# A mixer-and-FFN layer: another buffer for the recurrence's decay, another ring for the last pooling copies, a later place for one chunk's products

## The chip, the cores and the metric

The kernel runs on one core of one Trainium2 chip. Its engines run side by side, each through its own list of instructions in a fixed order: TensorE (PE, matrix products), VectorE (DVE), ScalarE (ACT), GpSimd (POOL, here mostly a queue for transfers) and SyncE (SP, a queue for transfers). [...] The metric is the time of one execution on the device in microseconds (us).

## The reference

One layer with 512 tokens and a width of 1024, in fp32:

```python
h = rms_norm(x, norm_mix)
proj = einsum('bsd,dc->bsc', h, w_in)
u_pool, u_lru, q, k, v, g_logits = split(proj)
gates = sigmoid(g_logits + b_gate)              # three branches
y_pool = pool_mixer(u_pool, w_pool, pool_scale) # causal means over 2, 4, 8, 16 tokens, minus the token
y_lru = rglru_mixer(u_lru, ...)
y_sb = stick_breaking_attention(rms(q), rms(k), v)   # 8 heads of 128
merged = sum over branches of gates[b] * (y_b @ w_branch[b])
x = x + merged @ w_out
h2 = rms_norm(x, norm_ffn)
x = x + (silu(h2 @ w_ffn_gate) * (h2 @ w_ffn_up)) @ w_ffn_down
```

The recurrence, which the first part of the change touches:

```python
xc = causal convolution of u_lru over 4 tokens
r, i = sigmoid(xb @ w_rg + b_rg), sigmoid(xb @ w_ig + b_ig)   # 16 blocks of 64
log_a = -8 * r * softplus(-lru_lambda)
a = exp(log_a)
mult = sqrt(-expm1(2 * log_a))
h[t] = a[t] * h[t-1] + mult[t] * (i * xc)[t]
```

## The kernel before

Channels lie on the 128 partitions, tokens along the free dimension, 512 of them. Every product in fp32 is made of three matmuls with operands that are split into a high and a low part (fp32r): high by high, high by low, low by high (`mm3`, L307 to L311). Weights are split on the chip: a load into `raw`, ACT copies it to `whi` (L141), DVE subtracts and leaves `wlo` (L142). `raw`, `whi` and `wlo` are rings of three buffers each, so the copy into a `whi` waits until PE has read the weight that stood there three loads before. For query, key and value, some gates, the branch products and the FFN a block product is made with seven products of sums of blocks instead of eight (the names 11, 12, S1, S2, S3, S4, 22); their sums of weights are made by DVE and are then split (L1442 and L1443 in the FFN).

A scheduler orders each engine's instructions from the order in which the program issues them, with priorities: `tc.high_priority(n)` moves what it encloses ahead in that order, as far as its operands and buffers allow. Small work is put in a list, `bg`, whose entries are taken out between the matmuls of a chunk by `tick`; so a `step` in the list is a place in the order, and the steps' contents are fixed by the lists below.

**The recurrence** (87 to 165 us of the span) has four chunks of 256 channels, each as [128, 2, 512]. `lru_chunk` gives four steps for each: the convolution, the split of its result (`xch` L653, `xcl` L654), the two gates on PE (`lg`, L664) with their tanh on ACT (L668 and L669, eight halves of 64 partitions), and `tanh` (DVE L673 for i times xc, ACT L676 for `lt`). With e = exp (in `lr`) and t = the tanh in `lt`, `lru_exp` takes the exponential and the square root, both on ACT; `lru_decay` makes the decay 1-(1+e)t, where the second half stands on DVE for chunks 0 and 1 and on ACT for 2 and 3; `lru_input` makes the scan's input (1+e)·root·i·xc with two products (L710, L711); `lru_scan` scans (L717) and `lru_store` splits and stores. Exponential and tanh need no change of ACT's function table between them; the square root needs a table load, and what follows it another. The buffers come from the ring "b" (13 of them). Between these steps PE works on `ps_lru`, on the second branch's gates (`ps_gate`) and, from about 130 us, on queries and keys (`ps_q`, L834) by seven products, with their weights `qw` and sums `qs` (L209, L217).

**The pooling mixer** (in the stage of about 345 to 363 us) has four groups, in the order 1, 0, 3, 2. `pool_chunk` multiplies, `evac_u` copies the two PSUM results to `up` (L980), `pool_mean` makes the windows by shifted sums on DVE (L988 to L994). Next to it run the attention's head by head: the transposes of a head's q and k (`pq`, L1056, whose result is split to `qkh` and `qkl`), the scores `z`, the weights' transposes (`pw`, split to `wth` L1108 and `wtl` L1109), and the product of pooled results with the first branch's weight (`ps_br`, merged by `m`, L410). These small tiles come from two rings: `slot` is used for working tiles and `slot_ld` (12 buffers) for what is loaded: the gates `g` and the heads' q, k and v (`at`, L1049), issued on SP's queue.

**The FFN** (after the output projection) makes its first two chunks of 256 hidden channels directly (gate `ps_fg`, up `ps_fu`) and the others with seven products (`seven`). As RMS is applied after the product, a direct chunk's result is silu(g·rb)·(u·rb), four instructions for each half: DVE L1513, ACT L1514, DVE L1515 and L1516. In `seven(2)` the plan's steps write two PSUM tiles, `ps_y` and `ps_x`; after a step a half of the tile is copied to `tx` or `ty` by ACT (L1495), and the next step that writes the same half waits for that. `make_a` has the weights of three steps ahead summed and split.

Of the kernel before, what the change touches and what calls it, by code (L numbers as in the profile page):

```python
# [17 lines left out]
S = 512  # L18
# [49 lines left out]
def layer_kernel(ctx: ExitStack, tc: tile.TileContext, x, xt, vecs, w_in, w_qkv7, w_gate7, w_pool, w_rg, w_ig,  # L68
# [16 lines left out]
    def b4(shape, name, tag="b", dt=F32):  # L85
        bufs = {"w": NAW, "t": NAT, "b": NAB}[tag]
        return pools["ap0"].tile([P] + shape, dt, tag=tag, name=name, bufs=bufs)
# [13 lines left out]
    def in_order(ap, b=H):  # L101
        w = ap.ndim == 3
        if b == H:
            return ap.rearrange("p w (b a) -> p w a b" if w else "p (b a) -> p a b", b=b)
        return ap.rearrange("p (c b a) -> p c a b", a=2, b=b)

    def two(ap, b=H):
        w = ap.ndim == 3
        if b == H:
            return ap.rearrange("p w (a b) -> p w a b" if w else "p (a b) -> p a b", b=b)  # L110
        return ap.rearrange("p (c a b) -> p c a b", a=2, b=b)
# [329 lines left out]
    with ExitStack() as first:  # L441
# [247 lines left out]
        def lru_exp(cs):  # L689
            for c in cs:  # L690
                for j in range(2):
                    r = lru[c]["r"][:, j, :]
                    ct = 2 * c + j
                    act(r, r, AF.Exp, scale=cneg[:, ct:ct + 1], bias=cneg[:, ct:ct + 1])
            for c in cs:
                lru[c]["s"] = b4([2, S], f"ls{c}")
                act(lru[c]["s"], lru[c]["t"], AF.Sqrt, scale=0.25)


        def lru_decay(c):  # L700
            e, t = lru[c]["r"], lru[c]["t"]
            dve.scalar_tensor_tensor(t, e, 1.0, t, ALU.add, ALU.mult)
            if c < 2:
                dve.tensor_scalar(t, t, -1.0, 1.0, ALU.mult, ALU.add)
            else:
                act(t, t, AF.Identity, scale=-1.0, bias=1.0)

        def lru_input(c):
            e, s_ = lru[c]["r"], lru[c]["s"]
            dve.scalar_tensor_tensor(s_, e, 1.0, s_, ALU.add, ALU.mult)  # L710
            dve.tensor_tensor(s_, s_, lru[c]["i"], ALU.mult)  # L711

        def lru_scan(c):
            t, s_ = lru[c]["t"], lru[c]["s"]
            h = lru[c]["i"]
            for j in range(2):
                dve.tensor_tensor_scan(h[:, j, :], t[:, j, :], s_[:, j, :], 0.0, ALU.mult, ALU.add)  # L717
            lru[c] = h
# [39 lines left out]
        def step(*fs):  # L758
            bg.append(lambda: [f() for f in fs])

        def of(f, c):
            return lambda: f(c)
# [3 lines left out]
        c1, s1, g1, t1 = lru_chunk(1)  # L766
        step(c1), step(s1), step(g0), step(t0)
        c2, s2, g2, t2 = lru_chunk(2)
        step(of(lru_exp, (0,))), step(c2), step(s2), step(g1)
        gate1(0)  # L770
        step(of(lru_decay, 0), t1), step(of(lru_exp, (1,))), step(g2), step(of(lru_input, 0))
        c3, s3, g3, t3 = lru_chunk(3)
        step(c3), step(s3), step(of(lru_decay, 1), of(lru_scan, 0)), step(t2, of(lru_input, 1))
        gate1(1)
        step(of(lru_scan, 1)), step(g3, of(lru_store, 0)), step(t3, of(lru_store, 1)), step(of(lru_exp, (2, 3)))
        gate1(2)
        for f, c in ((lru_decay, 2), (lru_decay, 3), (lru_input, 2)):
            step(of(f, c))
        bg.extend(prepare_t())
        gate1(3)  # L780

# [144 lines left out]
    def slot(name, dt=F32, shape=(S,)):  # L926
        return sp.tile([P] + list(shape), dt, tag="s", name=name, bufs=NSP - NLD)
# [14 lines left out]
    with ExitStack() as mix:  # L942
# [32 lines left out]
                dve.tensor_tensor(lo, r, hi.bitcast(F32), ALU.subtract)  # L975
                pool_w[2 * h + g] = (hi, lo)

        def evac_u(ps, name):
            u = slot(name)
            act(two(u), in_order(ps), AF.Copy)  # L980
            return u

        def pool_mean(g, j, u):
# [32 lines left out]

        def pool_chunk(g):
            pss = chan_chunk(("pool", g), hn, 1)
            us = [evac_u(pss[j], f"up{g}{j}") for j in range(2)]
            for j in range(2):  # L1020
                bg.append(lambda j=j, u=us[j]: pool_mean(g, j, u))
            if g != POOL[0]:
                queue_pool_back(POOL[POOL.index(g) - 1])
# [271 lines left out]
    with ExitStack() as ffn:  # L1295
# [171 lines left out]
        def finish_act(t, ps, a):  # L1467

            v = two2(t)
            dve.tensor_tensor(v, v, in_order2(ps), ALU.add)  # L1470
            act(t[:, 0, :], t[:, 0, :], AF.Silu)
            dve.tensor_tensor(a, t[:, 0, :], t[:, 1, :], ALU.mult)
# [4 lines left out]
        def seven(c):  # L1477
            a = g4([2, S], f"act{c}")
            tx, ty = g4([2, S], f"tx{c}"), g4([2, S], f"ty{c}")
            Y = fp.tile([P, 2, S], F32, tag="mm", name=f"ps_y{c}")  # L1480
            X = fp.tile([P, 2, S], F32, tag="mm", name=f"ps_x{c}")
            lo, hi = slice(0, H), slice(H, S)
            plan = (("11", Y, 1, True, tx, lo, Y, hi),
                    ("12", X, 0, True, None, None, None, None),
                    ("S2", Y, 1, False, tx, hi, Y, hi),
                    ("S1", X, 1, False, ty, hi, X, hi),
                    ("S3", Y, 1, False, ty, lo, Y, hi),
                    ("S4", X, 1, False, None, None, None, None),
                    ("22", Y, 0, False, None, None, None, None))
            n0 = steps.index((c, "11"))  # L1490
            for n, (nm, ps, half, first, t, ts_, src, ss) in enumerate(plan):
                make_a(n0 + n + 3)
                product(A.pop((c, nm)), B[0, WITH[nm]], ps, half, first, True)
                if t is not None:
                    act(two2(t[:, :, ts_]), in_order2(src[:, :, ss]), AF.Copy)  # L1495
                if c == DOWN - 1 and nm in PRE:
                    split_d2("11", PRE.index(nm), 0, 0)
                if nm == "S4":
                    finish_act(tx, X, a[:, 0, :])
                if nm == "22":  # L1500
                    finish_act(ty, Y, a[:, 1, :])
            acts.append(a)

        bg.extend([lambda: None, rms2] + prepare_b())
        for c in range(NDIRECT):
            pg = chan_chunk(("fg", c), h2, 3, fp)
            pu = chan_chunk(("fu", c), h2, 3, fp)
            if c == NDIRECT - 1:
                make_a(3)
            a = g4([2, S], f"act{c}")  # L1510
            for j in range(2):
                sg = small(f"sg{c}{j}", 2, "sq2")
                dve.tensor_tensor(two(sg), in_order(pg[j]), two(rb2), ALU.mult)  # L1513
                act(sg, sg, AF.Silu)  # L1514
                dve.tensor_tensor(two(sg), two(sg), in_order(pu[j]), ALU.mult)  # L1515
                dve.tensor_tensor(a[:, j, :], sg, rb2, ALU.mult)  # L1516
            acts.append(a)
        tick(len(bg))
        for c in range(NDIRECT, NF // 2):
            if c == NF // 2 - 1:  # L1520
                ah, al = g4([2, S], "ah", F32R), g4([2, S], "al", F32R)
                act(ah, acts[0], AF.Copy)
                dve.tensor_tensor(al, acts[0], ah.bitcast(F32), ALU.subtract)
            seven(c)
# [207 lines left out]
```

## Time and profile before

| | |
|---|---|
| median of three runs (lowest, highest) | 872.93 us (872.79, 872.95) |
| the profiled execution | 872.6 us |
| its span, from the first to the last instruction | 870.8 us |
| mean granted clock of TensorE | 1.000 |
| read from HBM, written | 132.71 MB, 18.87 MB |
| mean transfer rate over the span | 174 GB/s |

The page gives each engine's busy time and its share of the span, then the span in 40 slices, the chain of work that ended last, and the costliest groups of instructions. PE is the engine's matmuls, PEld its loads of weights, which overlap them. The chain that ended last goes through PE for 76% of the span, through DVE for 10%, ACT 6%, transfers 4%.

A row of the timeline reads: start in us from the span's start, duration, engine, line of the kernel, operation, output<-inputs, shape and type, count; a bracket gives the engine's idle time before it and what ended it. A count above 1 stands for neighbours of the same form, with their time together. The start of an operation to the start of the next on the same engine is shorter than its duration, since they overlap.

### The profile page before, as it was taken

What the parts mean: (1) busy time and instruction counts of PE and PEld (TensorE: products, weight loads), DVE (VectorE), ACT (ScalarE), POOL (GpSimd) and SP (SyncE); (2) the same over time, 40 slices, a digit from 0 to 9 for tenths busy, and PEclk for the clock granted to TensorE, in tenths of its full rate; (3) what the DMA queues carried; (4) which work ended last, traced back from release to release, by engine and by line L of the source; (5) the groups of instructions that cost most, each with busy time, mean ns of one, the idle gap of its engine ahead of it and who ended that gap; (6) DMA issues with size and microseconds to landing.
All of it is one profiled execution on the core that took longest, in us unless ns stands there. A gap on an engine that the chain in (4) does not pass through costs nothing.

```text
span 870.8 us, 14268 instructions
## 1 busy us (share of the span) xinstructions
PE 859.7 (99%) x5563; PEld 789.7 (91%) x5563; DVE 741.2 (85%) x961; ACT 522.1 (60%) x727; POOL 91.8 (11%) x130
## 2 busy tenths in 40 slices
PE   9999999999999999999999999999999999999998
PEld 7888878888899888889889998889999999999998
DVE  7899897998787699977898786699988888899974
ACT  6554989556856565565665545464555555755642
POOL 1110002232433101000001100000000000121200
PEclk9999999999999999999999999999999999999999
DMA  9686356799582786635736955345543343798913
GB/s 340 167 291 195 97 169 194 215 318 253 176 271 73 238 246 205 218 122 155 217 98 152 212 171 170 98 138 151 150 117 97 106 114 109 233 243 204 192 39 121
DMA packets 116643, 154.08 MB, mean 177 GB/s; under 512 B 8160, under 2 KB 90080, under 8 KB 116576
## 3 DMA queue, kind: packets, MB, share of 16 engines
q1 hardware_dynamic: 103904, 107.30, 38.5%
q0 software_dynamic: 12528, 45.62, 22.1%
q8 instruction: 43, 0.70, 0.3%
q10 hardware_dynamic: 144, 0.26, 0.1%
q14 instruction: 24, 0.20, 0.1%
HBM read 132.71 MB, written 18.87 MB: 174 GB/s over the span
## 4 chain that ended last, share of the span: by engine, by line
PE 76%; DVE 10%; ACT 6%; DMA 4%; issue 2%; SPq 1%; POOL 0%; ACTq 0%; DVEq 0%; POOLq 0%
PE ps_y L318 10%; PE ps_x L318 8%; PE ps_q L834 6%; PE ps_dy L1651 6%; PE ps_dx L1651 5%; DVE wlo L142 3%; PE ps_br L309 3%; PE ps_br L310 3%; PE ps_br L311 3%; PE ps_bY L1277 2%; PE ps_gate L737 2%; DMA qw<-in_w_gate_dram 2%; PE ps_bX L1277 2%; ACT whi L141 2%; PE ps_gy L318 2%
## 5 line engine op out<-in xcount | busy, mean ns | idle before, releaser
L141 ACT ACTIVATE whi<-raw 128x1024 fp32r<-128x1024 f32 x69 | 72.8, 1055 | 76.8 <-PE ps_out L310 16.0
L142 DVE TENSOR_TENSOR wlo<-raw,whi 128x1024 fp32r<-128x1024 f32 x69 | 84.2, 1220 | 23.6 <-ACT whi L141 23.0
L142 DVE TENSOR_TENSOR wlo<-qw,whi 128x1024 fp32r<-128x1024 f32 x48 | 58.4, 1219 | 17.3 <-ACT whi L141 17.1
L141 ACT ACTIVATE whi<-qw 128x1024 fp32r<-128x1024 f32 x48 | 50.4, 1052 | 29.9 <-PE ps_q L834 14.9
L1442 ACT ACTIVATE wh_S<-w_S 128x1024 fp32r<-128x1024 f32 x36 | 38.0, 1059 | 33.0 <-PE ps_y L318 19.9
L1555 POOL DMA_DIRECT2D dw<-in_w_down_dram x20 | 16.9, 862 | 306.3 <-DMA dw<-in_w_down_dram 263.8
L1443 DVE TENSOR_TENSOR wl_S<-w_S,wh_S 128x1024 fp32r<-128x1024 f32 x36 | 43.7, 1220 | 3.8 <-ACT wh_S L1442 3.8
L1442 ACT ACTIVATE wh<-w 128x1024 fp32r<-128x1024 f32 x27 | 28.6, 1058 | 26.9 <-issue 9.1
L1443 DVE TENSOR_TENSOR wl<-w,wh 128x1024 fp32r<-128x1024 f32 x27 | 32.9, 1220 | 8.4 <-ACT wh L1442 8.4
L1442 ACT ACTIVATE whdS<-dw 128x1024 fp32r<-128x1024 f32 x20 | 21.2, 1058 | 21.3 <-PE ps_dy L1651 10.6
L1443 DVE TENSOR_TENSOR wldS<-dw,whdS 128x1024 fp32r<-128x1024 f32 x20 | 24.2, 1220 | 5.5 <-ACT whdS L1442 5.5
L1093 DVE TENSOR_TENSOR_SCAN E<-K,ahead 128x512 f32<-128x512 f32 (+3 forms) x32 | 25.3, 812 | 3.9 <-ACT K L1089 3.9
L309 PE MATMUL ps_br<-yHH,whi 128*128 128x512 f32 x64 | 24.6, 385 | 1.4 <-ACT up L980 1.4
L309 PE MATMUL ps_lru<-HH,whi 128*128 128x512 f32 x64 | 24.6, 384 | 0.0
L309 PE MATMUL ps_br<-yph,whi 128*128 128x512 f32 x64 | 24.5, 383 | 0.0
L309 PE MATMUL ps_pool<-HH,whi 128*128 128x512 f32 x64 | 24.5, 383 | 0.0
L309 PE MATMUL ps_gate<-HH,whi 128*128 128x512 f32 x64 | 24.4, 381 | 0.0
L310 PE MATMUL ps_br<-ypl,whi 128*128 128x512 f32 x64 | 24.3, 379 | 0.0
L311 PE MATMUL ps_gate<-HH,wlo 128*128 128x512 f32 x64 | 24.3, 379 | 0.0
L310 PE MATMUL ps_gate<-HL,whi 128*128 128x512 f32 x64 | 24.3, 379 | 0.0
L310 PE MATMUL ps_br<-yHL,whi 128*128 128x512 f32 x64 | 24.3, 379 | 0.0
L311 PE MATMUL ps_br<-yHH,wlo 128*128 128x512 f32 x64 | 24.3, 379 | 0.0
(740 smaller groups left out, 3444.1 us busy)
## 6 DMA issues: line engine op xcount, KB each, us to landing
raw<-in_w_in_dram SPq DMA_DIRECT2D x31, 512.0 KB, 5.1
qw<-in_w_qkv_dram SPq DMA_DIRECT2D x24, 512.0 KB, 7.0
dw<-in_w_down_dram POOLq DMA_DIRECT2D x20, 512.0 KB, 7.6
w<-in_w_ffn_gate_dram SPq DMA_DIRECT2D x36, 256.0 KB, 3.6
w<-in_w_ffn_up_dram SPq DMA_DIRECT2D x36, 256.0 KB, 4.5
raw<-in_w_branch_dram SPq DMA_DIRECT2D x16, 512.0 KB, 3.9
qw<-in_w_qkv_dram POOLq DMA_DIRECT2D x12, 512.0 KB, 8.0
qd<-r POOLq DMA_DIRECT2D x12, 512.0 KB, 7.4
```

Source lines behind the costliest of these rows:

```text
L141: act(hi, raw, AF.Copy)
L142: dve.tensor_tensor(lo, raw, hi.bitcast(F32), ALU.subtract)
L309: nc.tensor.matmul(ps, lh, rh, start=start, stop=False, skip_group_check=skip)
L310: nc.tensor.matmul(ps, lh, rl, start=False, stop=False, skip_group_check=skip)
L311: nc.tensor.matmul(ps, ll, rh, start=False, stop=stop, skip_group_check=skip)
L318: nc.tensor.matmul(o, a_[a][:, w, k, :], il2(b_[b][:, k, :]), start=first and n == k == 0, stop=last and n == 2 and k == 3, skip_group_che ...
L834: nc.tensor.matmul(ps[:, a, :], b_[:, k, ts_], il(a_[:, kk, :]), start=first and n == k == 0, stop=n == 2 and k == 3, skip_group_check=True)
L1093: dve.tensor_tensor_scan(E[:, c0:c0 + n][:, ::-1], K[:, c0 + 1:c0 + n + 1][:, ::-1], ahead[:, S - n:][:, ::-1], 0.0, ALU.mult, ALU.add)
L1277: nc.tensor.matmul(o, ah[x_][:, w, k, :], il2(b[k][y_]), start=first_ and n == k == 0, stop=n == 2 and k == 3, skip_group_check=True)
L1442: act(h, src, AF.Copy)
L1443: dve.tensor_tensor(l, src, h.bitcast(F32), ALU.subtract)
L1651: nc.tensor.matmul(o, a_[a][:, w, k0 + k, :], il2(b_[b][:, k, :]), start=first and i == k == 0, stop=last and i == 2 and k == nk - 1, skip ...
```

## The change

There are three parts.

The recurrence. The square root becomes a function of its own, `lru_root`, and writes its result over t, where it was a new buffer before. `lru_decay` writes a new buffer `a`, where it was in place on t. `lru_input` and `lru_scan` take them from there. The steps are grouped anew: chunks 0 and 1 have exponential, decay and root in one step; for chunks 2 and 3 a step has both decays, the next both roots, the next the input of chunk 2.

The pooling copies. For the last group (2) `evac_u` takes its buffer from the ring of loads (`slot_ld`) and copies with `high_priority(EARLY)`, where EARLY is 300; the other groups are as before (a priority of 0).

The FFN. The four instructions for each half of the second direct chunk become a function, `direct_act`. For the first chunk it is called where they stood; for the second it is called from `seven(2)`, after the plan's steps 1 ("12") for the first half and 2 ("S2") for the second.

```diff
@@ lru_exp, lru_decay, lru_input, lru_scan
+        def lru_root(cs):
             for c in cs:
-                lru[c]["s"] = b4([2, S], f"ls{c}")
-                act(lru[c]["s"], lru[c]["t"], AF.Sqrt, scale=0.25)
+                act(lru[c]["t"], lru[c]["t"], AF.Sqrt, scale=0.25)
         def lru_decay(c):
             e, t = lru[c]["r"], lru[c]["t"]
-            dve.scalar_tensor_tensor(t, e, 1.0, t, ALU.add, ALU.mult)
+            a = lru[c]["a"] = b4([2, S], f"la{c}")
+            dve.scalar_tensor_tensor(a, e, 1.0, t, ALU.add, ALU.mult)
             if c < 2:
-                dve.tensor_scalar(t, t, -1.0, 1.0, ALU.mult, ALU.add)
+                dve.tensor_scalar(a, a, -1.0, 1.0, ALU.mult, ALU.add)
             else:
-                act(t, t, AF.Identity, scale=-1.0, bias=1.0)
+                act(a, a, AF.Identity, scale=-1.0, bias=1.0)
         def lru_input(c):
-            e, s_ = lru[c]["r"], lru[c]["s"]
+            e, s_ = lru[c]["r"], lru[c]["t"]
         def lru_scan(c):
-            t, s_ = lru[c]["t"], lru[c]["s"]
+            t, s_ = lru[c]["a"], lru[c]["t"]
@@ the steps
-        step(of(lru_exp, (0,))), step(c2), step(s2), step(g1)
+        step(of(lru_exp, (0,)), of(lru_decay, 0), of(lru_root, (0,))), step(c2), step(s2), step(g1)
         gate1(0)
-        step(of(lru_decay, 0), t1), step(of(lru_exp, (1,))), step(g2), step(of(lru_input, 0))
+        step(t1), step(of(lru_exp, (1,)), of(lru_decay, 1), of(lru_root, (1,))), step(g2), step(of(lru_input, 0))
         c3, s3, g3, t3 = lru_chunk(3)
-        step(c3), step(s3), step(of(lru_decay, 1), of(lru_scan, 0)), step(t2, of(lru_input, 1))
+        step(c3), step(s3), step(of(lru_scan, 0)), step(t2, of(lru_input, 1))
...
-        for f, c in ((lru_decay, 2), (lru_decay, 3), (lru_input, 2)):
-            step(of(f, c))
+        step(of(lru_decay, 2), of(lru_decay, 3)), step(of(lru_root, (2, 3))), step(of(lru_input, 2))
@@ evac_u, pool_chunk
-        def evac_u(ps, name):
-            u = slot(name)
-            act(two(u), in_order(ps), AF.Copy)
+        def evac_u(ps, name, last):
+            u = (slot_ld if last else slot)(name)
+            with tc.high_priority(EARLY if last else 0):
+                act(two(u), in_order(ps), AF.Copy)
             return u
-            us = [evac_u(pss[j], f"up{g}{j}") for j in range(2)]
+            us = [evac_u(pss[j], f"up{g}{j}", g == POOL[3]) for j in range(2)]
@@ seven, the direct chunks
+                if (c, n) in after:
+                    after[c, n]()
...
-            for j in range(2):
+
+            def direct_act(j, c=c, a=a, pg=pg, pu=pu):
                 sg = small(f"sg{c}{j}", 2, "sq2")
                 dve.tensor_tensor(two(sg), in_order(pg[j]), two(rb2), ALU.mult)
                 act(sg, sg, AF.Silu)
                 dve.tensor_tensor(two(sg), two(sg), in_order(pu[j]), ALU.mult)
                 dve.tensor_tensor(a[:, j, :], sg, rb2, ALU.mult)
+
+            if c < NDIRECT - 1:
+                direct_act(0), direct_act(1)
             acts.append(a)
         tick(len(bg))
+        after = {(NDIRECT, 1): lambda: direct_act(0), (NDIRECT, 2): lambda: direct_act(1)}
```

## The prediction

> **What bounds the kernel now.** I read the page's first lines, then the waits of TensorE (PE), then the timelines of PE, ScalarE (ACT) and VectorE (DVE) around the three places that the diff touches.
>
> ```profile
> span 870.8 us, 14268 instructions
> PE 859.7 (99%) x5563; PEld 789.7 (91%) x5563; DVE 741.2 (85%) x961; ACT 522.1 (60%) x727; POOL 91.8 (11%) x130
> PEclk9999999999999999999999999999999999999999
> ```
>
> PE is busy for 99% of the span at full clock, so the instructions on other engines cost only what they make PE wait. The diff leaves every engine the same number of instructions; what it alters is their order. So the question is which waits of PE go, which ones come, and where. The waits are few (columns: what PE waited with, for what, us in total, times, longest):
>
> ```profile
> PE ps_br L309 <- ACT up L980: 1.4, 1, 1.4
> PE lg L664 <- DVE xcl L654: 1.3, 1, 1.3
> PE ps_q L834 <- DVE wlo L142: 1.1, 3, 0.7
> PE ps_x L318 <- DVE wl_S L1443: 0.8, 1, 0.8
> PE pq L1056 <- DMA at<-qd: 0.2, 1, 0.2
> ```
>
> The first, second and fourth are the waits that the three edits stand beside: the pooling copies (up), the recurrence (xcl is the low part of its convolution), the FFN (wl_S). All that the change can gain is in these rows, about 4 us with the restart of the pipeline; a loss has no such ceiling.
>
> **The change part by part.**
>
> *A, the recurrence.* Before, Sqrt followed the exponentials at once and the decay came afterwards. Now the root overwrites t, so it must wait until DVE's decay has read t. Chunk 0 on ACT, before:
>
> ```profile
> 89.05 1.28 ACT L697 ACT_TABLE_LOAD   x1
> 90.35 1.06 ACT L697 ACTIVATE ls<-lt 128x1024 f32<-128x1024 f32 x1
> 91.31 1.04 ACT L141 ACTIVATE whi<-raw 128x1024 fp32r<-128x1024 f32 x1
> ...
> 93.66 0.68 ACT L668 ACTIVATE lr<-lg,brg 64x512 f32<-64x512 f32 x1
> ```
> ```profile
> 90.51 0.38 PE L310 MATMUL ps_gate<-HL,whi 128*128 128x512 f32 x1
> ```
>
> In the new order the weight copy whi stands between the exponentials and the table load. It reuses a buffer that PE reads until 90.51+0.38=90.89, a wait that the load and the Sqrt used to cover. So: whi 90.9 to 91.95, table load (1.28) to 93.2. Meanwhile DVE takes the weight's low part, one product of this chunk, then the decay, each 1.14 start to start and 1.22 long (rows below): 92.1, 93.2, 94.35, ending 95.6. Root (1.06) to 96.65, table load to 97.95. The first tanh of the next chunk thus starts at 97.95 instead of 93.66, 4.3 late. The gate matmuls of chunk 2 need the PSUM that these eight tanh empty; by the same walk they wait about 1.8 in three pieces (estimate). That costs nothing by itself, because the wait for xcl (1.3, and some 0.17 for the restart) stood right behind it: xcl for chunk 3 ends at the same time in both orders, 122.1.
>
> ```profile
> 120.86 1.22 DVE L654 TENSOR_TENSOR xcl<-xc,xch 128x1024 fp32r<-128x1024 f32 x1
> ...
> 143.56 1.22 DVE L142 TENSOR_TENSOR wlo<-qw,whi 128x1024 fp32r<-128x1024 f32 x1
> ...
> 145.83 1.22 DVE L142 TENSOR_TENSOR wlo<-qw,whi 128x1024 fp32r<-128x1024 f32 x1
> 146.96 2.35 DVE L209 TENSOR_TENSOR qw<-qw,qs 128x1024 f32<-128x1024 f32 x2
> ...
> 158.31 2.33 DVE L717 TENSOR_TENSOR_SCAN li<-lt,ls 128x512 f32<-128x512 f32 x2
> ```
>
> What stays is that ACT reaches the tanh of chunk 3 later, 124.3 (1.1 to 1.5 late by the walk) against 122.87:
>
> ```profile
> 122.87 0.68 ACT L668 ACTIVATE lr<-lg,brg 64x512 f32<-64x512 f32 x1 [0.46 <-PE lg L664]
> ...
> 132.74 2.92 ACT L694 ACTIVATE lr<-lr,cneg 128x512 f32<-128x512 f32 x4
> ...
> 141.24 0.69 ACT L606 ACTIVATE gt<-ps_gate,bhalf 128x512 f32<-128x512 f32 x1
> 141.82 1.05 ACT L141 ACTIVATE whi<-qw 128x1024 fp32r<-128x1024 f32 x1
> ...
> 143.34 1.06 ACT L706 ACTIVATE lt<-lt 128x1024 f32<-128x1024 f32 x1
> ```
>
> The four exponentials of chunks 2 and 3 then end at 132.74+2.92+1.4=137.1. Behind them now stand a gate tanh (0.58), a weight copy (0.95), another gate tanh (0.58) and the decay's second half (1.0), to 140.2; table load to 141.5; root of chunk 2 to 142.55. DVE's first product with that root runs 142.6 to 143.7, then the next weight's wlo at 143.7, nearly as before (143.56). But between that wlo and the next one the scheduler now puts four operations instead of one: second product of chunk 2, a sum of query weights, first product of chunk 3, one scan. Each takes 1.14 to 1.17 start to start (2.35 and 2.33 for two). So the second wlo starts at 143.7+5x1.14=149.4 instead of 145.83 and ends at 150.6.
>
> ```profile
> 147.31 0.38 PE L834 MATMUL ps_q<-whi,HH 128*128 128x512 f32 x1
> 147.52 0.38 PE L834 MATMUL ps_q<-wlo,HH 128*128 128x512 f32 x1
> 150.50 0.48 PE L834 MATMUL ps_q<-wlo,hT2h 128*128 128x512 f32 x1 [0.23 <-DVE wlo L142]
> 161.81 0.48 PE L834 MATMUL ps_q<-wlo,hT3h 128*128 128x512 f32 x1 [0.68 <-DVE wlo L142]
> ```
>
> PE used that wlo at 147.52; now it can at 150.65: +3.1, whatever happened to PE earlier. Part comes back: the two waits that followed, 0.23 and 0.68, are waits for the same queue, and DVE owes later what it has done early (the scans and products). Matmuls run 0.21 apart and last 0.38, so a wait of 0.23 costs 0.39 and one of 0.68 costs 0.84. 3.1-0.39-0.84 = **+1.9**. Low end: if ACT is not held up at the weight copy and stands at 122.87 as before, wlo ends 1.5 earlier: +0.4. High end: only the first wait is swallowed: +2.8. I take +1.9, since PE's own read at 90.51 holds the copy up.
>
> The root's destination is free of cost: the decay's new buffer takes the place of the root's old one in the same ring.
>
> *B, the pooling copies.*
>
> ```profile
> 349.77 0.48 PE L309 MATMUL ps_br<-yHH,whi 128*128 128x512 f32 x1 [1.43 <-ACT up L980]
> ...
> 356.97 1.04 PE L1056 MATMUL pq<-idn,at 128*128 128x128 f32 x8
> ...
> 362.35 0.28 PE L310 MATMUL z<-qkl,qkh 128*128 128x256 f32 x1
> ```
> ```profile
> 349.10 1.10 ACT L980 ACTIVATE up<-ps_pool 128x512 f32<-128x512 f32 x2
> ```
> ```profile
> 355.71 1.61 DVE L1109 TENSOR_TENSOR wtl<-pw,wth 128x512 fp32r<-128x512 f32 x3
> ...
> 359.82 0.68 DVE L410 SCALAR_TENSOR_TENSOR m<-g,ps_br 128x512 f32<-128x512 f32 x1
> 360.66 0.69 DVE L939 TENSOR_TENSOR p20l<-up,p20h 128x512 fp32r<-128x512 f32 x1 [0.16 <-ACT p20h L938]
> 361.47 0.75 DVE L1060 SCALAR_TENSOR_TENSOR qkl<-pq,qg,qkh 128x512 fp32r<-128x512 f32 x1
> ```
>
> PE waits 1.43 for these copies, as they stood behind seven other ACT instructions. They now come first, and the wait (1.6 with the restart) goes. But one copy (about half of 1.10, 0.48 after overlap) now delays a weight copy, and with it DVE, which has no gap from there to 360: the first wtl ends at 356.4+0.5=356.9. PE would be at its transposes at 356.97-1.6=355.4 and waits there for wtl, which frees the PSUM they write, until 356.9. Gain used up: 0. Behind that, a merge product (m, 0.68, 0.6 start to start) now stands ahead of the pooling result, so nothing covers ACT's copy p20h any more; 0.48+0.6, less the 0.16 that was idle before, makes qkl end at 363.15 instead of 362.22, and the scores' matmul at 362.35 reads it: **+0.8**. Low end: wtl is not late and m hides, -1.6. High end: the delay of 0.48 also shows at 356.97, +1.2. I take +0.8, as every step hangs on DVE being without a gap.
>
> The copies' new buffers belong to the ring of loads, so some loads on SP's queue (gates, one head's q, k, v) are issued behind one or two weight loads. The only wait of PE for such a load is 0.2; with all of it doubled the cost is 0.2, and I take nothing.
>
> *C, the FFN.* The products with 1/rms of the second direct chunk leave the time in which DVE must make the first sums of weights.
>
> ```profile
> 601.40 0.38 PE L318 MATMUL ps_x<-B0T1h,wh_S 128*128 128x256 f32 x1
> 602.66 0.38 PE L318 MATMUL ps_x<-B0T1h,wl_S 128*128 128x256 f32 x1 [0.77 <-DVE wl_S L1443]
> ```
> ```profile
> 602.20 0.58 ACT L1495 ACTIVATE tx<-ps_y 128x512 f32<-128x512 f32 x1
> 604.96 1.06 ACT L1442 ACTIVATE wh_S<-w_S 128x1024 fp32r<-128x1024 f32 x1 [2.19 <-DVE w_S L1424]
> ```
> ```profile
> 601.38 2.36 DVE L1443 TENSOR_TENSOR wl_S<-w_S,wh_S 128x1024 fp32r<-128x1024 f32 x2 [0.52 <-ACT wh_S L1442]
> ```
>
> The first of these two wl_S ended at 602.5. Its sum and its split now stand ahead of three products of the chunk's second half (0.6 each) and need not idle for 0.52, so it ends at about 600.2: the wait at 602.66 (0.94 with the restart) and a step of 0.29 ahead of 601.40 go, -1.2. In exchange the second copy tx<-ps_y now stands on ACT behind the split of the next sum (1.06), which waits for DVE until about 602.5: 603.55, then the copy (0.58) to 604.15, while PE wants that half of ps_y at 603.8: +0.35. Net **-0.85**. Ends: -1.3 with the copy in time; +0.2 if that sum comes one DVE operation (1.13) later.
>
> *Sum.* +1.9+0.8-0.85 = +1.85. The profiled execution took 872.6 (span 870.8 and 1.8 around it), the runs' median is 0.33 above it: 872.93+1.85 = 874.8.
>
> **The rivals.**
>
> *Faster.* DVE has more slack than my walk gives it, so every late link reaches PE in time: A +0.4, B -1.6, C -1.3, sum -2.5, 870.4. For it: DVE is busy 85% of the span and idles between the exponentials' stages. Against it: the orders are fixed, and the four operations ahead of the second wlo are there on every execution. It decides once DVE is more than 1.5 earlier than I have it at both 143.7 and 356.4.
>
> *The parts cancel.* ACT makes up its 4.3 before chunk 3, because there were idle pieces there (0.46 at 122.87 is one). Then A is +0.4 and the sum +0.35: 873.3.
>
> *Heavier.* DVE's backlog from the recurrence does not pay the later waits back, and the pooling delay shows twice: 2.8+1.2-0.3 = +3.7, 876.6.
>
> *The clock.* The page grants full clock in all 40 slices, across waits of up to 1.43. The new wait for wlo is longer, 3.1 in two pieces of about 0.9 and 2.2 (whi of that half splits it). If PE's clock halved for as long as that wait, the loss would be another 1.6, 876.4. [...]
>
> **How the numbers follow.** A measurement of this kernel can tell about 0.2% (1.75 us) from no change: faster below 871.2, slower above 874.7. Chances: forecast 0.48, of which 0.38 above 874.7 and 0.10 within; cancelling 0.17, within; heavier 0.13 and clock 0.04, both slower; faster 0.18. So slower 0.55, within 0.27, faster 0.18. The forecast's own range, with A between +1.1 and +2.8, is 874.0 to 875.8. The range that should hold 8 in 10 takes in cancelling and heavier and leaves out most of the faster case: 871.0 to 876.9.
>
> **What would show it.** Right: in PE's waits the rows for xcl, up and wl_S shrink or are gone; a wait for wlo of 2 to 3 us near 150 takes their place; Sqrt of chunk 0 starts near 95.6 with the tanh behind it near 98; one for qkl near 363. Wrong: no long wait for wlo between 143 and 152 (A falls, and with it the sign); PE at the transposes of head 3 more than 1 us earlier, measured from the stage's start (B falls); a copy of ps_y that is ready before 603.8 less the stages' shift (C gains 0.35). If a granted clock below full shows behind the wait for wlo, it is the clock.

## The result

The changed kernel takes 875.03 us, the median of 21 runs (872.72 to 878.31); before takes 872.93, the median of 21 runs (871.75 to 874.10). The ratio is 1.0026, with a 95% interval of 1.0018 to 1.0033: slower by some 2.1 us. The forecast was 874.8.

The profiled execution of the changed kernel took 874.87, its span 873.1. First lines of its page:

```profile
span 873.1 us, 14271 instructions
PE 862.0 (99%) x5563; PEld 790.9 (91%) x5563; DVE 741.7 (85%) x961; ACT 522.3 (60%) x727; POOL 91.2 (10%) x130
```

Busy times of DVE, ACT and POOL are those of before within 0.6. PE's is up by the span's 2.3, and some of that is matmuls that were stretched by a slower clock (below): there a matmul of the same form lasts 0.63 instead of 0.38, and PE counts as busy for 3.40 of 3.40 us. So the page says only that nothing was added. PE's waits say more (what PE waited with, for what, us in total, times, longest):

```profile
PE ps_q L835 <- DVE wlo L142: 1.8, 1, 1.8
...
PE lg L664 <- ACT li L669: 0.8, 1, 0.8
PE ps_q L835 <- ACT whi L141: 0.8, 1, 0.8
PE pq L1058 <- DVE wtl L1111: 0.7, 2, 0.5
PE ps_br L310 <- DMA yHL<-ydl: 0.7, 1, 0.7
```

The rows for up (1.4), xcl (1.3) and wl_S (0.8) are gone. In their place stand a wait for a weight's low part, one for its high part, one for the tanh, one for wtl, and one for a transfer.

PE's timeline shows what came of the longest of them:

```profile
148.34 0.48 PE L835 MATMUL ps_q<-whi,HH 128*128 128x512 f32 x1 [0.75 <-ACT whi L141]
150.61 0.48 PE L835 MATMUL ps_q<-wlo,HH 128*128 128x512 f32 x1 [1.78 <-DVE wlo L142]
150.93 0.38 PE L835 MATMUL ps_q<-whi,HL 128*128 128x512 f32 x1
...
152.34 0.63 PE L835 MATMUL ps_q<-wlo,HH 128*128 128x512 f32 x1
152.77 0.63 PE L835 MATMUL ps_q<-whi,HL 128*128 128x512 f32 x1
...
155.42 0.38 PE L835 MATMUL ps_q<-whi,hT2h 128*128 128x512 f32 x1
155.63 0.38 PE L835 MATMUL ps_q<-wlo,hT2h 128*128 128x512 f32 x1
```

The low part is there at 150.6. A microsecond behind it the starts are 0.43 apart instead of 0.21, and from 155.2 on 0.21 again. The windows around that stretch give the granted clock (columns: us, then busy time of PE, PEld, DVE, ACT, POOL with counts, granted clock, share of the DMA engines, GB/s):

```profile
147.50:150.60 3.10, 0.57 (x2) 0.19 (x1) 3.10 (x4) 3.10 (x4) 0.00 (x0) 1.00 0.10 19
150.60:151.70 1.10, 1.09 (x5) 0.99 (x6) 1.10 (x2) 1.07 (x2) 0.68 (x1) 0.98 0.00 0
151.70:155.10 3.40, 3.40 (x10) 2.68 (x9) 3.40 (x4) 0.38 (x1) 0.05 (x1) 0.51 0.40 154
155.10:158.50 3.40, 3.40 (x18) 2.97 (x17) 3.39 (x3) 1.62 (x2) 0.74 (x1) 1.00 0.20 76
```

For 3.4 us PE had half its clock. In 8 of the 21 runs the mean clock is 0.998 or 0.996 (median 876.45), in 13 it is 1.000 (median 874.88). One such stretch at half clock is 3.4 x 0.5 / 873 = 0.002 of the span, so by this estimate 0.998 is one of them and 0.996 two. By the medians the time splits accordingly: +1.95 where the clock held, 1.6 more where it dropped.

A second profile of the changed kernel (e12 below) has the clock at 1.000. The start of one and the same matmul, less its start in the profile of before, in us:

| matmul, by its start before | first profile | second profile |
|---|---|---|
| 6 (first gates) | +0.1 | +0.4 |
| 147.52 (wlo, the late low part) | +3.1 | +3.4 |
| 161.81 (wlo, the last wait of before) | +3.5 | +2.2 |
| 261.84 (gy, waited for gx) | +2.8 | +1.9 |
| 299.92 (waits for a head's load) | +2.6 | +2.2 |
| 349.77 (waited for up) | +1.0 | +0.6 |
| 355.89 (yHL) | +1.75 | +1.0 |
| 356.97 (transposes) | +2.6 | +2.1 |
| 362.57 (pps) | +3.0 | +2.5 |
| 375.64 (transposes of head 3's weights) | +3.2 | +2.8 |
| 602.66 (waited for wl_S) | +1.9 | +1.4 |
| 605.21 (waits for tx) | +2.2 | +1.7 |

The second column is the account at full clock: the recurrence +1.8 (2.2 less 0.4 from the start), the pooling stage +0.6 (2.2 to 2.8, in both columns), the FFN -1.1.

### The profile page after: what moved, and what is told of

Read it like the earlier page. It is cut to its first block, busy times and chain, and to the rows that moved or that the text cites. A ratio compares the mean times of both kernels' runs of the same rounds, so it can differ in the third digit from the quotient of the medians.

```text
span 873.1 us, 14271 instructions
## 1 busy us (share of the span) xinstructions
PE 862.0 (99%) x5563; PEld 790.9 (91%) x5563; DVE 741.7 (85%) x961; ACT 522.3 (60%) x727; POOL 91.2 (10%) x130
## 4 chain that ended last, share of the span: by engine, by line
PE 84%; DVE 7%; ACT 6%; issue 2%; DMA 1%; SPq 0%; ACTq 0%; DVEq 0%
PE ps_y L318 11%; PE ps_x L318 8%; PE ps_q L835 8%; PE ps_dy L1660 6%; PE ps_dx L1660 5%; PE ps_gy L318 2%; PE ps_bY L1279 2%; PE ps_gate L739 2%; PE ps_br L310 2%; PE ps_br L309 2%; PE ps_br L311 2%; PE ps_bX L1279 2%; PE ps_gx L318 2%; DVE wlo L142 2%; ACT whi L141 1%
## 5 line engine op out<-in xcount | busy, mean ns | idle before, releaser
L311 PE MATMUL ps_lru<-HH,wlo 128*128 128x512 f32 x64 | 24.4, 381 | 0.0
L311 PE MATMUL ps_br<-yph,wlo 128*128 128x512 f32 x64 | 24.3, 379 | 0.0
L311 PE MATMUL ps_pool<-HH,wlo 128*128 128x512 f32 x64 | 24.3, 379 | 0.0
```

Of the source, the lines that this page charges most:

```text
L311: nc.tensor.matmul(ps, ll, rh, start=False, stop=stop, skip_group_check=skip)
```

## The experiments

Each kernel was compared with before on the same chip: e1 to e4 on one, e5 to e12 on another. All times are medians of so many runs.

| | what differs | us (runs) | before | ratio, 95% interval | lowest clock |
|---|---|---|---|---|---|
| e1 | the recurrence's part alone | 875.39 (12) | 873.21 | 1.0025, 1.0014 to 1.0037 | 0.996 |
| e2 | the pooling part alone | 873.52 (11) | 873.21 | 1.0003, 0.9995 to 1.0012 | 0.999 |
| e3 | the FFN's part alone | 872.07 (12) | 873.21 | 0.9988, 0.9979 to 0.9997 | 0.999 |
| e4 | all, PE kept busy in the wait | 875.67 (8) | 873.21 | 1.0024, 1.0014 to 1.0034 | 1.000 |
| e5 | recurrence, chunks 0 and 1 alone | 875.64 (6) | 872.88 | 1.0032, 1.0019 to 1.0044 | 0.999 |
| e6 | recurrence, chunks 2 and 3 alone | 872.31 (11) | 872.88 | 0.9993, 0.9985 to 1.0002 | 1.000 |
| e7 | all, high parts first in one block | 874.23 (11) | 872.88 | 1.0019, 1.0010 to 1.0028 | 1.000 |
| e8 | one pooling copy ahead, alone | 872.31 (11) | 872.88 | 0.9998, 0.9989 to 1.0007 | 0.999 |
| e9 | all but the recurrence's part | 872.42 (12) | 873.06 | 0.9997, 0.9988 to 1.0006 | 0.999 |
| e10 | e8 and later FFN products | 871.55 (11) | 873.06 | 0.9985, 0.9977 to 0.9994 | 0.999 |
| e11 | e10 and e6 | 870.80 (12) | 873.06 | 0.9978, 0.9969 to 0.9986 | 0.999 |
| e12 | the changed kernel again | 874.41 (1) | 873.06 | | 1.000 |

Before's own clock in the 88 runs beside these was never under 0.999.

**The parts alone: e1, e2, e3, e9.** Each takes some hunks of the change and leaves the others as before: e1 those from `lru_exp` to the steps, e2 `evac_u` and `pool_chunk`, e3 `seven` and the direct chunks, e9 the last two together:

```diff
@@ e1 has this; e2, e3 and e9 don't
-        step(of(lru_exp, (0,))), step(c2), step(s2), step(g1)
+        step(of(lru_exp, (0,)), of(lru_decay, 0), of(lru_root, (0,))), step(c2), step(s2), step(g1)
@@ e2 and e9 have this; e1 and e3 don't
-            us = [evac_u(pss[j], f"up{g}{j}") for j in range(2)]
+            us = [evac_u(pss[j], f"up{g}{j}", g == POOL[3]) for j in range(2)]
@@ e3 and e9 have this; e1 and e2 don't
+        after = {(NDIRECT, 1): lambda: direct_act(0), (NDIRECT, 2): lambda: direct_act(1)}
```

> The recurrence's part of the change alone. Theory 1 (the late low part of a weight behind four VectorE operations): the wait near 150.6 is there as in the changed kernel, PE is +3.1 at that matmul, about +1.9 at 165 where the clock holds and about +3.5 where it drops behind the wait; some 0.7 is given back at the later wait for gx. End: +1.1 to +2.8, median about +2. Rival (the loss comes from the pooling stage, whose transfers moved): within 0.5 of before.

> The pooling copies alone. Theory 1: the wait for up (1.6 with its restart) goes and is used up at the transposes by a wait for wtl; behind it +0.4 to +0.8; end +0.4 to +0.8. Rival (a transfer, the wait of 0.7 for yHL that the changed kernel shows near 357, is this part's real cost): that wait is there here too, and the end is +0.8 or more. Second rival (the copies ahead are a plain gain): -1.6.

> The later products in the FFN alone. Theory 1: the two steps at 601.4 and 602.7 (1.2 together) go, the late copy of ps_y gives some 0.3 back; end -0.8 to -1.1. Rival (the gain in the changed kernel is only lateness that the stage takes up): within 0.3 of before.

> The change without its recurrence part: pooling copies and later products, as in the changed kernel. Theory 1 (the recurrence makes the whole loss): no wait above 0.9 between 143 and 165, clock 0.999 to 1.000, end -0.3 to -0.9. Rival (the parts depend on each other: with the recurrence on time the pooling stage pays more): 0 to +0.8.

The recurrence alone gives +2.2 by the medians, as much as the whole change. Its waits, in a profile at full clock:

```profile
PE ps_q L835 <- DVE wlo L142: 1.8, 1, 1.8
...
PE ps_br L309 <- ACT up L981: 1.4, 1, 1.4
PE lg L664 <- ACT li L669: 0.8, 1, 0.8
PE ps_x L318 <- DVE wl_S L1444: 0.8, 1, 0.8
PE ps_q L835 <- ACT whi L141: 0.8, 1, 0.8
```

The wait for wlo is there, those for up and wl_S as before; PE is +3.4 at the late low part, +2.1 at 161.81 and +1.4 at gy. 6 of its 12 runs are at 0.998 or below (median 876.08), the other 6 at 1.000 (874.28, so +1.1). The pooling part alone is +0.3 by the medians and can't be told from before; its profile has PE at -0.3 ahead of the stage, -1.9 where it waited for up, -0.3 at the transposes, +0.1 at pps and +0.3 at 375.64, so the stage is +0.6, as inside the change. In this one PE lost no more than 0.14 to the transfer yHL, so that transfer isn't the stage's price. The FFN alone gains 1.1 by the medians: PE is -0.2 ahead of the stage, -1.5 at the first wl_S, -1.2 behind the copy. Without the recurrence's part the rest lies -0.3 (ratio) to -0.6 (medians) from before, which can't be told from no change; its profile has the pooling stage at +0.6 again (from -0.3 to +0.3) and the FFN at -1.1. The three parts alone sum to 2.2+0.3-1.1 = +1.4 against +2.1 measured together; the intervals are wide enough for that.

**Two halves of the recurrence: e5, e6.** In each, two chunks keep root and decay as before, the other two have the new order.

```diff
@@ e5, against the recurrence's part: chunks 2 and 3 as before
+        OLD = (2, 3)
...
+                if c in OLD:
+                    lru[c]["s"] = b4([2, S], f"ls{c}")
+                else:
+                    lru[c]["s"] = lru[c]["t"]
...
+            a = lru[c]["a"] = t if c in OLD else b4([2, S], f"la{c}")
...
-        ... step(of(lru_exp, (2, 3)))
+        ... step(of(lru_exp, (2, 3)), of(lru_root, (2, 3)))
-        step(of(lru_decay, 2), of(lru_decay, 3)), step(of(lru_root, (2, 3))), step(of(lru_input, 2))
+        step(of(lru_decay, 2)), step(of(lru_decay, 3)), step(of(lru_input, 2))
@@ e6: OLD = (0, 1), with the steps of chunks 0 and 1 as before
```

> The recurrence's part for chunks 0 and 1 alone; chunks 2 and 3 have root and decay as before. Theory 1 (root behind decay holds ScalarE up in chunks 0 and 1, and that lateness is what arrives at the low parts of the query weights): waits of 0.8 to 1.0 at the gates' matmul near 105, then no single wait of 1.78 near 150.6 but two of 1.5 to 2 at low parts near 146 and 164; end +2 to +2.8, the clock at 1.000 in nearly all runs, since the waits lie 18 apart. Rival (the order of chunks 2 and 3 makes the loss): within 0.5 of before.

> The recurrence's part for chunks 2 and 3 alone. Theory 1: ScalarE comes to the exponentials in time, so the root of chunk 2 is there some 1.4 earlier and no wait above 0.9 stands between 143 and 165; end -0.7 to +0.2, clock 1.000 in all runs. Rival (four VectorE operations ahead of the second low part cost 3.1 whatever ScalarE did before): a wait of 1.5 to 1.8 near 150, end +1 to +2.

```profile
PE ps_q L841 <- DVE wlo L142: 3.5, 3, 1.8
```
```profile
164.55 0.48 PE L841 MATMUL ps_q<-wlo,hT3h 128*128 128x512 f32 x1 [1.80 <-DVE wlo L142]
```

That is e5: 3.5 in three waits, the longest at 164.55, and +2.7 at 161.81, more than with the whole recurrence's part. Its end is +2.8 (medians). VectorE's order there is that of before, with one product between the two low parts (145.18 and 147.45, before 143.56 and 145.83), and all of it 1.6 later. e6 is the other way: no wait for wlo above 0.2, two waits of 1.0 together for ACT's copy of ps_q where before has one of 0.4, PE at -0.3 at 161.81, and an end 0.6 below before by the medians with an interval that still holds zero. (Its profile is one of its longer executions, 873.64: PE goes to +1.0 by 299.92, with waits of 0.8 for gx and 0.8 for a head's load.) So the loss comes from chunks 0 and 1, where ScalarE stands until VectorE has made the decay. Moving the decay ahead of the root in chunks 2 and 3 costs nothing by itself when ScalarE arrives in time; the scheduler then also puts two operations between those low parts, and not the changed kernel's four. How much of ScalarE's lateness is the copy's wait, the root's wait or the uncovered table loads, no run separates.

**The clock: e4, e7, e12.** e4 puts matmuls with zeros into the wait; e7 changes the order of the block's twelve matmuls.

```diff
@@ e4, behind the matmul that starts the block (zero is [128, 128] bf16)
+        FILL = 8
...
+                            if (t, nm, i, a, kk, n) == (VKQ[0], "12", 1, 0, 0, 0):
+                                for _ in range(FILL):
+                                    nc.tensor.matmul(ps[:, a, :], zero, warm, start=False, stop=False,
+                                                     skip_group_check=True)
@@ e7
+                low = (t, nm, i) == (VKQ[0], "12", 1)
+                for a, kk, n in ([(a, kk, n) for n in (0, 2, 1) for a in range(2) for kk in range(2)] if low else
+                                 [(a, kk, n) for a in range(2) for kk in range(2) for n in range(3)]):
```

> The whole change, and behind the first matmul with the weight whose low part is late, eight matmuls with a stationary operand of zeros, which add nothing to the sum. They last 1.73 and fit into the wait of 1.78. Theory 1 (PE's idle time in the wait makes the clock drop): the low part still ends near 150.6, the matmuls behind it run 0.216 apart, the granted clock is 1.000 in every run, and no run is above about 876; median 874 to 874.9. Rival (the drop has another cause, or is there by chance): some runs at 0.998 or less as in the changed kernel (8 of 21 there), with times up to 878.

> The whole change, and in the block whose low part is late PE does the eight matmuls with the high part first and the four with the low part behind them. Theory 1: the wait of 1.78 shrinks to some 0.3, PE's idle time falls into pieces that no longer drop the clock: 1.000 in all runs, none above 876.5. Of the wait's 1.5 most comes back as a wait for the next low part, which VectorE makes later in the same queue, so the median is only 0.3 to 0.8 below the changed kernel's (874.2 to 874.7). Rival (the matmul order sets the loss): 873.3, the whole 1.5 gained.

> The changed kernel again, for a profile of another execution. Theory 1: the wait of 1.8 for the low part near 150.6 is there whatever the clock does; if the clock holds, the matmuls behind it run 0.216 apart, PE is +1.9 to +2.2 at 165 instead of +3.5, and the later waits (gx, the transfer of yHL) come out larger or smaller by what PE is earlier, so that the end is within 1.5 of the first profile's. Rival (the wait itself comes and goes with the clock): no wait above 1 there.

e4's timeline:

```profile
149.24 0.48 PE L838 MATMUL ps_q<-whi,HH 128*128 128x512 f32 x1 [0.75 <-ACT whi L141]
149.79 1.68 PE L843 MATMUL ps_q<-warm,zero 128*128 128x512 bf16 x7
151.51 0.48 PE L838 MATMUL ps_q<-wlo,HH 128*128 128x512 f32 x1
151.83 0.38 PE L838 MATMUL ps_q<-whi,HL 128*128 128x512 f32 x1
152.04 0.38 PE L838 MATMUL ps_q<-whi,HH 128*128 128x512 f32 x1
```

Seven of the eight added matmuls are in the trace. The low part comes no sooner (+4.0 in this execution, of which 1.0 is from a slower start ahead of 8 us), the matmuls behind it run 0.21 apart, and the clock is 1.000 in all 8 runs. In e1 and the changed kernel 14 of 33 runs dropped (in e1, on e4's chip, 6 of 12); eight in a row without a drop have a chance of (19/33)^8 = 1% if nothing had changed. None of the 8 is above 876.25. The median, though, missed: 875.67 where 874 to 874.9 was expected. VectorE's order differs too: two scans stand further ahead in its queue (at 155.91), and the trace shows a new wait of 1.00 for a low part at 160.55. That the scheduler reckons with the added matmuls would explain it; no run tests that. So by e4 the drop hangs here on PE's idle time in the wait: with 1.68 us of matmuls in it, none of 8 runs has one. It isn't a better kernel.

e7 fills the wait with the block's own matmuls: the clock is 1.000 in 11 of 11 runs, the wait for the low part is down to two of 1.2 together, and the next low part is late instead (PE is +2.2 ahead of it and +2.9 at it). The end is 874.23, within the expected 874.2 to 874.7; most of the 1.5 comes back as expected, and the kernel remains slower than before. On e7's chip the changed kernel itself ran only once (e12, at 1.000), so e7's clock alone says less than e4's.

e12 has the wait of 1.77 at full clock: it doesn't come with the drop. The drop comes with it, in some executions.

**The pooling copy and a better version: e8, e10, e11.**

```diff
@@ e8, from the changed kernel's pooling part, without the other two
-            us = [evac_u(pss[j], f"up{g}{j}", g == POOL[3]) for j in range(2)]
+            us = [evac_u(pss[j], f"up{g}{j}", g == POOL[3] and j == 0) for j in range(2)]
@@ e10, e8 and the FFN's part with
-        after = {(NDIRECT, 1): lambda: direct_act(0), (NDIRECT, 2): lambda: direct_act(1)}
+        after = {(NDIRECT, 1): lambda: direct_act(0), (NDIRECT, 3): lambda: direct_act(1)}
@@ e11, e10 and e6
```

> Before, with only the first of the two pooling copies in the ring of loads and at the higher priority; the second one stays where it was. VectorE's order is then that of before. Theory 1 (the second copy, ahead of a weight's copy, makes VectorE late by 0.48 and draws the merge product ahead): the wait for up goes, wtl at the transposes takes back about 1.1, and nothing is late behind it: end -0.3 to -0.5. Rival (the first copy alone makes wtl late by as much): 0 to +0.5, as with both.

> Before, with one pooling copy ahead and with the later products called after steps 1 and 3 of the plan instead of 1 and 2. Theory 1: the gains of the two add, -0.3 to -0.6 and -1.0 to -1.2, so 871.1 to 871.6 where before is 872.9. Rival (the FFN takes up what the pooling stage gains): -1.1 alone, 871.8.

> The same, and the recurrence's part for chunks 2 and 3 alone. Theory 1: some -0.2 more, which a measurement can hardly tell: 870.9 to 871.5. Rival (lateness of a block of query weights eats it): as without it.

e8's waits:

```profile
PE ps_br L310 <- DMA yHL<-ydl: 0.9, 1, 0.9
...
PE pq L1057 <- DVE wtl L1110: 0.2, 1, 0.2
```

The wait for up goes, wtl is in time, and what takes most of it back is not what was expected (wtl) but the transfer yHL: PE is at -0.3 ahead of the stage, -2.0 where it waited for up, -1.0 at yHL and -0.8 from the transposes on, so -0.5 in all. By the medians the kernel is 0.6 faster, by the ratio nothing that can be told from no change. e10 gains 1.5 by the medians; e11 gains 2.3, with an interval of 0.9969 to 0.9986: 870.8, the fastest here and clear of both kernels. Its waits:

```profile
PE lg L664 <- DVE xcl L654: 1.3, 1, 1.3
PE ps_q L841 <- ACT r L854: 1.0, 2, 0.6
PE ps_br L310 <- DMA yHL<-ydl: 0.8, 1, 0.8
```

The waits for up, for wl_S and all but 0.2 of those for wlo are gone; xcl's wait stays, since it is the changed order in chunks 0 and 1 that fills it, at a higher price. What e6's part adds beside e10 (0.75 by the medians) is more than the 0.2 that was expected; a direct comparison of the two was not made.

## Why the prediction was right, point by point

**The recurrence, up to the late low part: right, link by link, in the changed kernel.** ScalarE in chunk 0, after:

```profile
90.97 1.06 ACT L141 ACTIVATE whi<-raw 128x1024 fp32r<-128x1024 f32 x1 [1.88 <-PE ps_gate L310]
92.04 1.28 ACT L698 ACT_TABLE_LOAD   x1
95.63 1.07 ACT L698 ACTIVATE lt<-lt 128x1024 f32<-128x1024 f32 x1 [2.30 <-DVE la L704]
96.71 1.28 ACT L668 ACT_TABLE_LOAD   x1
98.01 0.68 ACT L668 ACTIVATE lr<-lg,brg 64x512 f32<-64x512 f32 x1
```

The copy waits 1.88 for PE's read of its buffer, the root 2.30 for the decay, and the first tanh is at 98.0 (97.95 by the sum). The new order puts both pieces of idle time, and the two table loads that used to lie in their cover, into ScalarE's path one behind the other. VectorE, where the loss lands:

```profile
143.68 1.22 DVE L142 TENSOR_TENSOR wlo<-qw,whi 128x1024 fp32r<-128x1024 f32 x1
144.81 1.22 DVE L713 TENSOR_TENSOR lt<-lt,li 128x1024 f32<-128x1024 f32 x1
145.95 1.22 DVE L209 TENSOR_TENSOR qw<-qw,qs 128x1024 f32<-128x1024 f32 x1
147.08 1.22 DVE L712 SCALAR_TENSOR_TENSOR lt<-lr,lt 128x1024 f32<-128x1024 f32 x1
148.22 1.22 DVE L719 TENSOR_TENSOR_SCAN li<-la,lt 128x512 f32<-128x512 f32 x1
149.35 1.20 DVE L142 TENSOR_TENSOR wlo<-qw,whi 128x1024 fp32r<-128x1024 f32 x1
```

149.35 where the sum had 149.4, and PE's matmul at 150.61 where it had 150.65. In the profile at full clock the two later waits give back 3.40-2.16 = 1.24; the sum had 0.39+0.84. The gates' waits ahead of that cost PE 1.9 by 117 us (1.8 in the estimate), and the gap that before has for xcl and a later one of 0.21 took all but 0.1 of it by 144.83. The rival in which ScalarE makes up its lateness is refuted by the exponentials' end at 137.1, and e5 and e6 show that this lateness decides. The four operations between the two low parts, which the sum needed for its +3.1, are there as read, but they aren't a cause of their own: e5 loses at least as much with one operation there. And the low end of +0.4, for a ScalarE that isn't held up, was too high: e6 shows no loss.

**The clock: given 4 in 100, and there in 8 of 21 runs.** Its price came out (1.6 forecast, 876.45-874.88 = 1.6 by the medians), partly by luck: it was reckoned as half of a wait of 3.1, and no run shows a half clock that lasts as long as the wait; in the changed kernel's first profile it lasts 3.4 behind a wait of 1.78, and 3.1 and 3.4 are nearly the same. Its chance did not come out. That 4 in 100 was the author's estimate, with no run behind it; it took the wait piece by piece, as 0.9 and 2.2. PE was idle for 0.75+1.78 = 2.5 with one matmul between, inside some 3 us, in both profiles of the kernel (0.76+1.77 in the second), and the clock dropped behind it in the first and held in the second.

The traces show where the clock changed. In the changed kernel's first profile the record of the granted clock has its first entry at 4.87, the fall at 151.65, 43 times 3.413 later, and the rise at 155.06, once more 3.41. In before's profile the first entry is at 4.92 and the fall, behind the kernel's end, at 871.90, 254 times 3.413 later. So in these two traces the clock changed only at the ends of stretches of 3.41, counted from the first entry. The stretch that ended at 151.65, and those of the second profile and of e5 that hold the long wait (columns as above):

```profile
148.23:151.65 3.42, 1.53 (x6) 1.13 (x7) 3.42 (x5) 3.42 (x5) 0.63 (x1) 1.00 0.03 6
149.08:152.49 3.41, 1.64 (x8) 1.41 (x8) 3.41 (x4) 2.92 (x4) 0.74 (x1) 1.00 0.01 1
162.47:165.89 3.42, 1.62 (x8) 1.21 (x7) 3.42 (x4) 1.97 (x2) 1.81 (x2) 1.00 0.29 38
```

PE was idle for 1.89 of the first, and the clock fell at its end. In the second profile the wait of 0.76 fell into the stretch before, 1.77 was left, and the clock held, as it did behind the 1.80 of e5. But idle time in such a stretch does not settle it: in the first profile PE is idle for 1.93 of the stretch from 868.45 to 871.86, and the clock is at 1.00 from there to the span's end at 873.09. Only one fall in mid-kernel is in a trace, so what decides between a drop and none, from one execution to the next, is not shown.

**The pooling stage: right in sum and sign, two links off.** Forecast +0.8, measured +0.6 over the stage in each of the six profiles that have this part (both of the changed kernel, e2, e4, e7, e9). PE's two waits that take back the gain at up:

```profile
357.64 0.48 PE L310 MATMUL ps_br<-yHL,whi 128*128 128x512 f32 x1 [0.70 <-DMA yHL<-ydl]
...
359.54 1.12 PE L1058 MATMUL pq<-idn,at 128*128 128x128 f32 x8 [0.55 <-DVE wtl L1111]
```

The gain was used up at the transposes as said (-1.6 to 0). But in the changed kernel the transfer yHL took part of it first: it landed at 357.60 there and at 354.47 before, where PE read it at 355.89, so that 1.42 was to spare, less than the wait that the change removes. The prediction had looked only at loads whose place in a queue moves, not at a transfer that PE would now meet earlier. And the late split qkl,

```profile
364.15 0.69 DVE L940 TENSOR_TENSOR p20l<-up,p20h 128x512 fp32r<-128x512 f32 x1 [0.70 <-ACT p20h L939]
364.76 0.74 DVE L1062 SCALAR_TENSOR_TENSOR qkl<-pq,qg,qkh 128x512 fp32r<-128x512 f32 x1
```

ends at 365.50, which is 0.7 later than before once PE's shift of 2.56 is taken off; idle in front of p20l, which m had covered, is 0.70 as against 0.16. The matmul that waits for it is pps at 365.56 (0.18), not the scores' one that was named: those read another head's split. (pps takes its PSUM from the same ring of three buffers as pq, which qkl reads.) Since pps had 0.35 to spare before, +0.4 is left of the +0.8; the restart behind the wait adds 0.1, and another 0.14, which stands in no row of waits, comes at 375.64.

**The FFN: right.** Forecast -0.85, measured -1.1 with the late copy of ps_y costing 0.27 of the 0.35 that was reckoned:

```profile
607.39 0.38 PE L318 MATMUL ps_y<-B0T3h,wh_S 128*128 128x256 f32 x1 [0.22 <-ACT tx L1497]
```

**The sum: right by two errors of opposite sign.** At full clock the stages add up to 1.8+0.6-1.1 = +1.3, against +1.85 forecast; the drops of the clock, 1.6 in 8 of 21 runs, add 0.6 on average. That is +1.9 where the medians say +2.1. The median of the 13 runs at full clock lies at +1.95, though, and not at +1.3. Their mean is at +1.5 (874.36 less 872.82, the mean of before's 21), which is near the account; single runs of before cover 2.3, and what is left between stays open. PE's wait for gx at 261.84 is no term of the change: PE comes out 0.3 to 0.7 better there than in before's profile in e2, e3, e8 and e9 too, which leave all that is ahead of it as it was, so that wait differs from execution to execution.

## What to carry to other kernels

Where an in-place update puts one engine's step behind another's read, count what stands on the waiting engine at that moment: here a copy that waits for a ring buffer and two table loads lost their cover, ScalarE was 4.3 us late, and the 1.4 of it that was left at the exponentials came back as waits of PE some 50 us on. Before a wait is taken away, look for every transfer and copy behind it that has less to spare than the wait is long, since PE will now meet them; and call a wait's removal a gain only where the next engine in line has a gap. And where a change brings idle pieces of PE close together, look at the granted clock too: here 0.75 and 1.78 with one matmul between went with a half clock of 3.4 us in the profile that has a drop, and 8 of 21 runs had one, while e5, whose longest wait is 1.80, had none in 6.

## What the runs showed of the hardware

In the changed kernel's first profile the clock dropped behind idle pieces that are shorter than the stretch of half clock that followed: 1.89 us idle within 3.42, out of 2.5 in two pieces, then 3.4 us at 0.51. In that trace and in before's it changed only at whole multiples of 3.413 us from its first entry in the record (43 and 44, and 254). A single wait of 1.8 (e5) did not do it in 6 runs, nor did waits of 1.4 and 1.3 that lie apart in 88 runs of before. Three runs are at 0.996, which by the same arithmetic is two such stretches (877.99, 878.31 and 879.61); where the second lies, no trace shows. And the first gates' matmuls, ahead of 8 us, start up to 0.9 later (e10) in kernels that are the same up to there. In before the clock's first entry is at 4.92, in e10 at 6.83. In before's profile the nine matmuls that start ahead of that entry (`warm_ps`) take 3.81 from 1.46 on, some 0.4 each, and the gates' matmuls start 0.21 apart from 5.82 on. That may be a good part of the 2.3 us over which before's own runs are spread; the runs don't show how much.
